# Attention in blocks of 256, 128, 128, 128, 128 and 256 tokens instead of four of 256, in a two-layer mLSTM and retention trunk

## The chip, the core and the metric

The kernel runs on one core of a Trainium2 chip. The metric is the device time of one execution in microseconds (us); the time before is the median of three runs.

## The reference, cut

Each of two layers normalises `x` (1024 tokens, width 1024), projects it with one wide matrix, runs eight heads of width 256 side by side (four mLSTM heads, four retention heads), gates and joins their outputs, and projects back onto `x`.

```python
h = rmsnorm(x, norm_g[l]) * (1.0 + scale) + shift
p = h @ w_in[l]                                   # q, k, v, gates of all heads
# mLSTM head, a step over a block of tokens j:
s   = einsum(q_j, k_j) * w_intra                  # scores inside the block, causal
num = einsum(s, v_j) + w_inter * einsum(C, q_j)   # inside the block + the state
den = sum(s) + w_inter * einsum(n, q_j)
h_j = num / maximum(abs(den), exp(-m_row))
C   = decay * C + einsum(w_end, v_j, k_j)         # the state goes to the next block
# retention head: the same with fixed decays gamma^(t-s), and no den
y   = concat(y_m, y_r) @ w_out[l]
x   = x + gate * y
```

The result does not depend on the size of the blocks. A larger block has more scores and fewer state updates.

## The kernel before

**Products.** All products are made of two halves of each operand, a high part H and a low part L. `mm3` (L133 to L136) issues three matmuls for one product: H by H (L134), L by H (L135) and H by L (L136). The halves are made by `split_to` (ScalarE writes the high part at L602; VectorE or GpSimd the low part at L603).

**Order of the work.** TensorE executes in the order of the program; the order on the other engines is made by a scheduler. The projections are cut into units of 12 matmuls with 512 columns. `run_units` issues one unit after another, and after each it gives one step (a tick) to the generators that are due, among them `attention` of the head whose projections are ready. So the attention of a head is laid between the projections of the next, a tick at a time. The projections accumulate in the PSUM pool `pp`, the attention in the pool `pa` (`ps_a()`, four tiles of 128 x 512 in f32).

**Attention of one head.** There are four blocks of CH = 256 tokens, each of two tiles of P = 128. `kT` and `qT` hold the transposed keys and queries, `kt` the key rows, `vs` the values, each as a pair of halves. For each block j:

- `scores(j)` (from L747): ten matmuls into one tile `ps`. Six make keys of the first tile by queries of both (256 columns). Four make the diagonal of the second tile (L760): one half of the keys by the two halves of the queries side by side, which gives two parts of 128 columns that are added later. VectorE multiplies both parts by the decay mask `dmat` (L762, L763), adds the two parts of the diagonal (L765), and the result is split into `sH` and `sL`. mLSTM heads make the mask from a row that is loaded (`dm_load`), cut by GpSimd and put through an exponential (`dm_make`); retention heads have a constant one, `rmask`.
- `values(j)` (L792): for each tile, the queries by the state (`cH`, `cL`, written by the update before; for j = 0 there is none), and the scores by the values. Then the normalisation of the head's output, in small VectorE, GpSimd and ScalarE steps.
- `update(j)` (L772), for j = 0, 1, 2: the new part of the state, twelve matmuls; VectorE adds it to the decayed state `cf` (L788), ScalarE and VectorE split that into `cH` and `cL`. There is one buffer of each.
- `finish(j)`: the transpose and the stores.

The order of the ticks is: loads of the masks, masks, `scores(0)`, `scores(1)`, and then for each j: `values(j)`; `update(j)`; `scores(j+2)`; `finish(j)`. A tick stands between each two. In all there are 16 heads (eight in each of two layers).

**Gates.** `gate_chain` makes, once in each layer, the columns `wi`, `we` and `dc` that weigh state and keys of the mLSTM heads, from the running maximum at the end of each block, which is loaded with one DMA into `ME` (L500) and subtracted on VectorE (L520 to L522).

Of the kernel before, what the change touches and what calls it, by code (L numbers as in the profile page):

```python
# [35 lines left out]
BIG = 1e30  # L36
GAMMA = [1.0 - 2.0 ** (-5.0 - h) for h in range(NH)]
# [32 lines left out]
def tile_hybrid_trunk(ctx, tc, x, c, positions, w_ada, b_ada, norm_g, w_in, conv_w, conv_b,  # L70
# [367 lines left out]
    def gate_chain(l, pgs, gt):  # L438
# [59 lines left out]
        ME = wt("ME", 16, 1)  # L498
        M4 = ME.rearrange("p (h j) -> p h j", h=4)
        Q.dma_start(M4, mdr[l].rearrange("h (j c) -> h j c", c=CH)[:, :, CH - 1:CH].rearrange("h j o -> o h j")  # L500
                    .to_broadcast([P, 4, 4]))
# [13 lines left out]
        wi = wd[:, 0:24].rearrange("p (h j t) -> p h j t", h=4, j=3)  # L515
        we = wd[:, 24:48].rearrange("p (h j t) -> p h j t", h=4, j=3)
        dc = wd[:, 48:56].rearrange("p (h j) -> p h j", h=4)
        for h in range(NH):
            me = M4[:, h, 0:3].unsqueeze(2).to_broadcast([P, 3, 2])
            V.tensor_tensor(wi[:, h], me, C4[:, 2:8, 2, h].rearrange("p (j t) -> p j t", t=2), ALU.subtract)  # L520
            V.tensor_tensor(we[:, h], C4[:, 0:6, 0, h].rearrange("p (j t) -> p j t", t=2), me, ALU.subtract)
        V.tensor_tensor(dc, M4[:, :, 0:2], M4[:, :, 1:3], ALU.subtract)  # L522
        A.activation(wd[:, 0:56], wd[:, 0:56], AF.Exp)
# [53 lines left out]
    def v_split(hg, gt, src, j):  # L577
        h, ml = hg % 4, hg < 4
        vH, vL = bt(F32R, 516), bt(F32R, 516)
        vH3 = vH.rearrange("p (a b) -> p a b", a=2)  # L580
        vL3 = vL.rearrange("p (a b) -> p a b", a=2)
        for tt in range(2):
            o = src[:, tt * HD:(tt + 1) * HD]
            if ml:
                s = gt["eul4"][:, h, 2 * j + tt, 0:1]
            else:
                s = kc[:, C_GS + 2 * h + tt:C_GS + 2 * h + tt + 1]
            A.activation(vH3[:, tt, 0:HD], o, AF.Copy, scale=s)
            V.scalar_tensor_tensor(vL3[:, tt, 0:HD], o, s, f(vH3[:, tt, 0:HD]), ALU.mult, ALU.subtract)
        if ml:  # L590
            for dst, src in ((vH3, gt["eH"]), (vL3, gt["eL"])):
                V.tensor_copy(dst[:, :, HD:HD + 2],
                              f(src.rearrange("p (h t o) -> p h t o", h=4, o=2)[:, h, 2 * j:2 * j + 2, :]))
        return vH3, vL3
# [41 lines left out]
    def k_rows(l, hg, j, kt, gt):  # L636
        h, ml = hg % 4, hg < 4
        half = j // 2
        a = 2 if half else 4
        kr = wt("acc", 512, 4)  # L640
        src = kdr[l][hg][half].rearrange("(b i) t -> i b t", i=32)
        for tb in range(4):
            o = tb * a * 32 + (j % 2) * 64
            Q.dma_start(kr[tb * 32:(tb + 1) * 32, :].rearrange("i (b c) -> i b c", c=64), src[:, :, o:o + 64])
        yield 2
        k3 = kr.rearrange("p (b t c) -> p t b c", t=2, c=32)
        kH, kL = bt(F32R), bt(F32R)
        kt[j] = (kH.rearrange("p (a b) -> p a b", a=2), kL.rearrange("p (a b) -> p a b", a=2))
        if ml:
            for tt in range(2):  # L650
                s = gt["we"][:, h, j, tt:tt + 1]
                dH, dL = (x[:, tt, :].rearrange("p (b c) -> p b c", c=32) for x in kt[j])
                A.activation(dH, k3[:, tt], AF.Copy, scale=s)
                V.scalar_tensor_tensor(dL, k3[:, tt], s, f(dH), ALU.mult, ALU.subtract)
        else:
            gw = float(np.float32(GAMMA[h] ** CH))
# [67 lines left out]
    def attention(l, hg, gt, qT, kT, kt, vs, gp, rot):  # L724
# [8 lines left out]
        def dm_load(j):  # L733
            if ml and j < NCH:
                dm = dms[j] = wt("dm", 512, 2)[:, 0:384]
                Q.dma_start(dm[:, 0:256], mdr[l][h:h + 1, j * CH:(j + 1) * CH].to_broadcast([P, CH]))
                Q.dma_start(dm[:, 256:384], mdr[l][h:h + 1, j * CH + P:(j + 1) * CH].to_broadcast([P, P]))

        def dm_make(j):
            if ml and j < NCH:  # L740
                dm = dms[j]
                G.affine_select(dm[:, 0:256], dm[:, 0:256], [[1, 256]], ALU.is_ge, BIG, base=0, channel_multiplier=-1)
                G.affine_select(dm[:, 256:384], dm[:, 256:384], [[1, 128]], ALU.is_ge, BIG, base=0, channel_multiplier=-1)
                for tt, sl in ((0, slice(0, 256)), (1, slice(256, 384))):
                    A.activation(dm[:, sl], dm[:, sl], AF.Exp, scale=-1.0, bias=gt["C4"][:, 2 * j + tt, 0, h:h + 1])

        def scores(j):  # L747
# [3 lines left out]
            pd = ps[:, CH:2 * CH].rearrange("p (a b) -> p a b", a=2)  # L751
            for dt in range(2):
                kk, qq = kT[dt][half], qT[dt][j]
                ks = slice(jo, jo + P)
                mm3(ps[:, 0:CH], (kk[0][:, ks], kk[1][:, ks]), (qq[:, 0:CH], qq[:, CH:2 * CH]), dt == 0, dt == 1)
            for dt in range(2):
                kk = kT[dt][half]
                qd = qT[dt][j].rearrange("p (a b) -> p a b", a=2)[:, :, P:CH]
                for i in range(2):
                    PE.matmul(pd, kk[i][:, jo + P:jo + CH], qd, start=dt == 0 and i == 0, stop=dt == 1 and i == 1)  # L760
            sd = wt("th", 512, 5)
            V.tensor_tensor(sd[:, 0:CH], ps[:, 0:CH], dmat[:, 0:CH], ALU.mult)  # L762
            V.tensor_tensor(sd[:, CH:2 * CH].rearrange("p (a b) -> p a b", a=2), pd,  # L763
                            dmat[:, CH:CH + P].unsqueeze(1).to_broadcast([P, 2, P]), ALU.mult)
            V.tensor_tensor(sd[:, CH:CH + P], sd[:, CH:CH + P], sd[:, CH + P:2 * CH], ALU.add)  # L765
            sd = sd[:, 0:CH + P]
            sH, sL = wt("sH", 384, 2, F32R), wt("sL", 384, 2, F32R)
            split_to((sH, sL), sd)
            sds[j] = (sH, sL)
            dm_load(j + 2)  # L770

        def update(j):  # L772
            if j == 0:
# [3 lines left out]
            new = (cH.rearrange("p (a b) -> p a b", a=2), cL.rearrange("p (a b) -> p a b", a=2))  # L777
            for dt in range(2):
                pu = ps_a()
                for tt in range(2):  # L780
                    kk = kt[j]
                    mm3(pu[:, 0:W], (kk[0][:, tt, dt * P:(dt + 1) * P], kk[1][:, tt, dt * P:(dt + 1) * P]),
                        (vs[j][0][:, tt, 0:W], vs[j][1][:, tt, 0:W]), tt == 0, tt == 1)
                if j == 0:
                    A.copy(cf[:, dt, 0:W], pu[:, 0:W])
                else:
                    dec = gt["dc"][:, h, j - 1:j] if ml else float(np.float32(GAMMA[h] ** CH))
# [4 lines left out]
        def values(j):  # L792
            half, jo = j // 2, (j % 2) * CH
            state = st["state"]
            sH, sL = sds[j]
            nd3 = wt("nd", 516, 1).rearrange("p (a b) -> p a b", a=2) if ml else None
            src = []
            for tt in range(2):
                pi = None
                if j > 0:  # L800
                    pi = ps_a()
                    for dt in range(2):
                        qq = qT[dt][j]
                        mm3(pi[:, 0:W], (qq[:, tt * P:(tt + 1) * P], qq[:, CH + tt * P:CH + (tt + 1) * P]), (state[0][:, dt, 0:W], state[1][:, dt, 0:W]),
                            dt == 0, ml and dt == 1)
                    if ml:
                        A.activation(nd3[:, tt, 0:W], pi[:, 0:W], AF.Copy, scale=gt["wi"][:, h, j - 1, tt:tt + 1])
                acc = not ml and j > 0
                po = pi if acc else ps_a()
                for si in range(tt + 1):  # L810
                    so = (tt * P if si == 0 else 256)
                    mm3(po[:, 0:W], (sH[:, so:so + P], sL[:, so:so + P]),
                        (vs[j][0][:, si, 0:W], vs[j][1][:, si, 0:W]), si == 0 and not acc, si == tt)
                if ml:
# [4 lines left out]
                    src.append(nd3[:, tt, 0:HD])  # L819
                else:  # L820
                    src.append(po[:, 0:HD])

            st6 = wt("st6", 12, 2)
            mv = wt("mv", 4, 2)
            mv3 = mv.rearrange("p (a b) -> p a b", a=2)
            for tt in range(2):
                V.bn_stats(st6[:, 6 * tt:6 * tt + 6], src[tt])
                V.bn_aggr(mv3[:, tt, :], st6[:, 6 * tt:6 * tt + 6])
            va = wt("va", 2, 2)
            rs = wt("rsd", 2, 2)  # L830
            if ml:
                den = nd3[:, :, HD]
# [9 lines left out]
            else:  # L842
                V.tensor_tensor(va, mv3[:, :, 1], kc[:, C_EPS + 2 * h:C_EPS + 2 * h + 2], ALU.add)
                G.tensor_tensor(rs, va, mhalf[:, 0:2], ALU.pow)
            nmu = wt("nmu", 2, 2)
            V.scalar_tensor_tensor(nmu, mv3[:, :, 0], -1.0, rs, ALU.mult, ALU.mult)
            n3 = wt("n", 512, 1).rearrange("p (a b) -> p a b", a=2)
            for tt in range(2):
                A.activation(n3[:, tt, :], src[tt], AF.Identity, scale=rs[:, tt:tt + 1], bias=nmu[:, tt:tt + 1])
            nrm[j] = n3  # L850
# [27 lines left out]
        for j in range(NCH):  # L878
            values(j)
            yield 1  # L880
            dm_make(j + 2)
            if j < NCH - 1:
                update(j)
# [3 lines left out]
            yield 1  # L887
            finish(j)
# [360 lines left out]
```

## Time and profile before

| What | Value |
|---|---|
| Time, median of three runs | 2331.36 us (2330.65 to 2338.51) |
| The profiled execution: time / span on the core | 2335.7 us / 2334.0 us |
| TensorE matmul: busy, share, instructions | 2293.4 us, 98%, 12589 |
| VectorE: busy, share, instructions | 1304.7 us, 56%, 2747 |
| ScalarE: busy, share, instructions | 889.3 us, 38%, 1736 |
| GpSimd: busy, share, instructions | 825.8 us, 35%, 801 |
| DMA | 260.50 MB, mean 112 GB/s |

In the profile PE is TensorE's matmuls, PEld its weight loads, DVE is VectorE, ACT ScalarE, POOL GpSimd and SP the engine that issues most DMAs. A row of the timeline has the start in us from the beginning of the span, the duration in us, the engine, the line of the kernel, the operation, the output and the input, the shape and the count; a square bracket holds the time that the engine stood idle before it and what ended the idle. A row of groups has the busy time in us, the mean of one instruction in ns, and behind the bar the idle time before them. A row of waits has the instruction that waited, what ended the wait, the sum in us, how often, and the longest. The span holds idle and busy time of each engine; the time of the execution is the span and a little around it.

### The profile page before, as it was taken

The page shows a single profiled execution, that of the slowest core. Times are in us where ns is not written, and L with a number is a line of the kernel's source. Part 1 is how long each engine was busy: PE and PEld are TensorE (multiplying, and loading weights), DVE is VectorE, ACT ScalarE, POOL GpSimd, SP SyncE. Part 2 cuts the span into 40 slices and gives each one's busy share as a digit, 9 for nine tenths or more (in the row PEclk, how much of TensorE's full clock was granted, in tenths as well). Part 3 has the DMA queues.
Part 4 walks back from the last instruction along what each step waited for, and adds up shares of the span by engine and source line. Part 5 has one row for each costly group of instructions (what it writes and reads, how often), then busy time and mean ns, then how long its engine had stood idle before and what let it go on. Part 6 is the DMA issues. An engine that isn't in the chain of part 4 may idle for free.

```text
span 2334.0 us, 34387 instructions
## 1 busy us (share of the span) xinstructions
PE 2293.4 (98%) x12589; PEld 1975.6 (85%) x12589; DVE 1304.7 (56%) x2747; ACT 889.3 (38%) x1736; POOL 825.8 (35%) x801
## 2 busy tenths in 40 slices
PE   6999999999999999999999999999999999999998
PEld 4888888889988888888888889888898888988886
DVE  7476687556554555574536655454553444556753
ACT  5535433433332323343434544343343322324432
POOL 1344333433333334222552434233334333341313
PEclk9999999999999999999999999999999999999999
DMA  7223332324442533385532332323223233435762
GB/s 254 76 67 95 78 84 75 97 65 116 121 115 76 149 84 96 119 261 198 179 89 61 82 77 75 84 73 76 75 71 95 73 91 86 131 90 180 263 203 81
DMA packets 326970, 260.50 MB, mean 112 GB/s; under 512 B 75892, under 2 KB 262012, under 8 KB 326800
## 3 DMA queue, kind: packets, MB, share of 16 engines
q1 hardware_dynamic: 326800, 258.30, 38.3%
q8 instruction: 99, 1.62, 0.3%
q14 instruction: 71, 0.58, 0.1%
HBM read 202.61 MB, written 55.61 MB: 111 GB/s over the span
## 4 chain that ended last, share of the span: by engine, by line
PE 87%; DVE 4%; DMA 3%; issue 2%; POOL 2%; ACT 1%; SPq 1%; POOLq 0%; ACTq 0%; DVEq 0%
PE pp L134 22%; PE pp L136 22%; PE pp L135 22%; PE pa L136 6%; PE pa L134 6%; PE pa L135 6%; PE pa L760 1%; DMA b<-in_w_ada_dram 1%; POOL wL L603 1%; DMA raw<-in_w_in_dram 1%; POOL b L603 1%; DVE acc L620 1%; DMA b<-in_x_dram 0%; POOL sL L603 0%; PE pa L304 0%
## 5 line engine op out<-in xcount | busy, mean ns | idle before, releaser
L134 PE MATMUL pp<-b,wH 128*128 128x512 f32 x1776 | 704.4, 397 | 1.8 <-ACT b L1093 1.8
L135 PE MATMUL pp<-b,wH 128*128 128x512 f32 x1776 | 701.2, 395 | 1.7 <-DVE b L1096 1.7
L136 PE MATMUL pp<-b,wL 128*128 128x512 f32 x1776 | 701.3, 395 | 0.6 <-POOL wL L603 0.6
L603 POOL TENSOR_TENSOR wL<-raw,wH 128x512 fp32r<-128x512 f32 x338 | 449.5, 1337 | 562.2 <-ACT wH L602 517.3
L136 PEld LDWEIGHTS pp<-b,wL 128*128 128x128 f32 x1776 | 334.8, 189 | 80.3 <-POOL wL L603 1.5
L135 PEld LDWEIGHTS pp<-b,wH 128*128 128x128 f32 x1776 | 334.7, 188 | 73.7 <-DVE b L1096 3.3
L134 PEld LDWEIGHTS pp<-b,wH 128*128 128x128 f32 x1776 | 334.9, 189 | 72.5 <-ACT b L1093 2.7
L602 ACT CAST wH<-raw 128x512 fp32r<-128x512 f32 x402 | 246.2, 617 | 381.5 <-PE pp L136 116.3
L134 PE MATMUL pp<-wH,b 128*128 128x256 f32 (+1 forms) x1152 | 352.7, 306 | 0.0
L136 PE MATMUL pp<-wH,b 128*128 128x256 f32 (+1 forms) x1152 | 352.3, 306 | 0.0
L135 PE MATMUL pp<-wL,b 128*128 128x256 f32 (+1 forms) x1152 | 352.3, 306 | 0.0
L603 POOL TENSOR_TENSOR b<-acc,b 128x256 fp32r<-128x256 f32 (+1 forms) x208 | 202.2, 992 | 337.0 <-ACT b L602 321.9
L136 PEld LDWEIGHTS pp<-wH,b 128*128 128x128 f32 x1152 | 216.5, 188 | 11.5
L134 PEld LDWEIGHTS pp<-wH,b 128*128 128x128 f32 x1152 | 216.9, 188 | 10.8
L135 PEld LDWEIGHTS pp<-wL,b 128*128 128x128 f32 x1152 | 216.7, 188 | 10.9
L602 ACT CAST b<-acc 128x256 fp32r<-128x256 f32 (+1 forms) x208 | 93.7, 487 | 193.6 <-DVE acc L697 138.7
L620 DVE SCALAR_TENSOR_TENSOR acc<-pp,cols,acc 128x511 f32<-128x511 f32 (+2 forms) x192 | 142.7, 743 | 44.2 <-ACT acc L615 42.0
L603 POOL TENSOR_TENSOR sL<-th,sH 128x384 fp32r<-128x384 f32 x64 | 67.8, 1059 | 249.4 <-ACT sH L602 148.9
L134 PE MATMUL pa<-wH,b 128*128 128x512 f32 x256 | 101.1, 395 | 0.0
L136 PE MATMUL pa<-wH,b 128*128 128x512 f32 x256 | 100.9, 394 | 0.0
L135 PE MATMUL pa<-wL,b 128*128 128x512 f32 x256 | 100.9, 394 | 0.0
L624 ACT ACTIVATE th<-acc 128x512 f32<-128x512 f32 x64 | 40.5, 632 | 148.6 <-DVE acc L622 76.7
(249 smaller groups left out, 3447.5 us busy)
## 6 DMA issues: line engine op xcount, KB each, us to landing
raw<-in_w_in_dram SPq DMA_DIRECT2D x274, 256.0 KB
raw<-in_w_out_dram SPq DMA_DIRECT2D x128, 256.0 KB
gdr<-g SPq DMA_DIRECT2D x64, 256.0 KB
ndr<-zt SPq DMA_DIRECT2D x128, 128.0 KB
raw<-in_w_ada_dram SPq DMA_DIRECT2D x64, 256.0 KB
g<-gdr SPq DMA_DIRECT2D x64, 256.0 KB
acc<-ndr SPq DMA_DIRECT2D x64, 256.0 KB
acc<-kdr SPq DMA_DIRECT2D x192, 64.0 KB
```

Of the source, the lines that this page charges most:

```text
L134: PE.matmul(o, lt[0], rt[0], start=start, stop=False)
L135: PE.matmul(o, lt[0], rt[1], start=False, stop=False)
L136: PE.matmul(o, lt[1], rt[0], start=False, stop=stop)
L602: A.copy(dst[0], src)
L603: eng.tensor_tensor(dst[1], src, f(dst[0]), ALU.subtract)
L620: V.scalar_tensor_tensor(acc[:, d:], pt[:, 0:HALF - d], wcol, acc[:, d:], ALU.mult, ALU.add)
L624: A.activation(th, acc, AF.Tanh, scale=0.5)
L760: PE.matmul(pd, kk[i][:, jo + P:jo + CH], qd, start=dt == 0 and i == 0, stop=dt == 1 and i == 1)
```

## The change

Blocks 0 and 3 stay whole (`WHOLE`). Blocks 1 and 2 are treated as two blocks of 128 tokens each, so that there are six blocks in a head.

- The score tile between the two halves of blocks 1 and 2 is not made; the second half takes the first from the state instead. Both halves of such a block are diagonals, of four matmuls each, into the two halves of one `ps` tile; the multiply by the mask follows each diagonal, then come two adds.
- `update` takes a tuple of tiles and is called five times in a head: for both tiles of block 0, and for each tile of blocks 1 and 2.
- `values` and the normalisation take the tiles of their block together or one by one. For blocks 1 and 2 the order of the ticks is: `values` of the first tile and its `update`; `scores(j+2)`; `values` of the second tile and its `update`; `finish(j)`. The number of ticks is the same.
- The gate columns are made for each tile of 128 instead of each block of 256 (`ME` has 32 columns instead of 16), the exponential of `wd` runs over 64 columns instead of 56, with five VectorE subtractions in place of nine. The second piece of the mask row is loaded only for whole blocks, and the mask of a split block is 128 + 128 columns instead of 256 + 128.
- The constant weights of keys, values and normalisation in the retention heads follow the shorter blocks (`place`, `span`).

```diff
+WHOLE = (0, 3)
+
+def place(t):
+    return t % 2 if t // 2 in WHOLE else 0
+
+def span(j):
+    return CH if j in WHOLE else P
...
-        ME = wt("ME", 16, 1)
+        ME = wt("ME", 32, 1)
...
-        for h in range(NH):
-            me = M4[:, h, 0:3].unsqueeze(2).to_broadcast([P, 3, 2])
-            V.tensor_tensor(wi[:, h], me, C4[:, 2:8, 2, h].rearrange("p (j t) -> p j t", t=2), ALU.subtract)
-            V.tensor_tensor(we[:, h], C4[:, 0:6, 0, h].rearrange("p (j t) -> p j t", t=2), me, ALU.subtract)
-        V.tensor_tensor(dc, M4[:, :, 0:2], M4[:, :, 1:3], ALU.subtract)
-        A.activation(wd[:, 0:56], wd[:, 0:56], AF.Exp)
+        V.tensor_tensor(wi[:, :, 0:5], M4[:, :, 1:6], peak[:, :, 2:7], ALU.subtract)
+        V.tensor_tensor(wi[:, :, 5:6], M4[:, :, 5:6], peak[:, :, 7:8], ALU.subtract)
+        V.tensor_tensor(we[:, :, 0:1], low[:, :, 0:1], M4[:, :, 1:2], ALU.subtract)
+        V.tensor_tensor(we[:, :, 1:6], low[:, :, 1:6], M4[:, :, 1:6], ALU.subtract)
+        V.tensor_tensor(dc, M4[:, :, 1:5], M4[:, :, 2:6], ALU.subtract)
+        A.activation(wd, wd, AF.Exp)
...
-                Q.dma_start(dm[:, 256:384], mdr[l][h:h + 1, j * CH + P:(j + 1) * CH].to_broadcast([P, P]))
+                if j in WHOLE:
+                    Q.dma_start(dm[:, 256:384], mdr[l][h:h + 1, j * CH + P:(j + 1) * CH].to_broadcast([P, P]))
...
+        def diagonal(pd, j, tt):
+            o = (j % 2) * CH + tt * P
+            for dt in range(2):
+                kk = kT[dt][j // 2]
+                qd = qT[dt][j].rearrange("p (a b) -> p a b", a=2)[:, :, tt * P:(tt + 1) * P]
+                for i in range(2):
+                    PE.matmul(pd, kk[i][:, o:o + P], qd, start=dt == 0 and i == 0, stop=dt == 1 and i == 1)
...
         def scores(j):
             ps = ps_a()
             sd = wt("th", 512, 5)
             if j in WHOLE:
...
+            else:
+                s4 = sd.rearrange("p (t a b) -> p t a b", t=2, a=2)
+                for tt in range(2):
+                    pd = ps[:, tt * CH:(tt + 1) * CH].rearrange("p (a b) -> p a b", a=2)
+                    diagonal(pd, j, tt)
+                    m = dmat[:, tt * P:(tt + 1) * P] if ml else dmat[:, CH:CH + P]
+                    V.tensor_tensor(s4[:, tt], pd, m.unsqueeze(1).to_broadcast([P, 2, P]), ALU.mult)
+                s3 = sd[:, 0:CH].rearrange("p (t b) -> p t b", t=2)
+                V.tensor_tensor(s3[:, 0], s4[:, 0, 0], s4[:, 0, 1], ALU.add)
+                V.tensor_tensor(s3[:, 1], s4[:, 1, 0], s4[:, 1, 1], ALU.add)
+                n = CH
...
-        def update(j):
+        def update(tiles):
...
-                for tt in range(2):
+                for t in tiles:
...
-                    dec = gt["dc"][:, h, j - 1:j] if ml else float(np.float32(GAMMA[h] ** CH))
+                    dec = gt["dc"][:, h, tiles[0] - 2:tiles[0] - 1] if ml else float(np.float32(GAMMA[h] ** P))
...
-        def values(j):
+        def values(j, tts):
...
+                sources = [(tt, tt * P)]
+                if j in WHOLE:
+                    sources = [(si, 256 if si else tt * P) for si in range(tt + 1)]
...
         for j in range(NCH):
-            values(j)
-            yield 1
+            whole = j in WHOLE
+            values(j, (0, 1) if whole else (0,))
+            if whole:
+                yield 1
             dm_make(j + 2)
             if j < NCH - 1:
-                update(j)
+                update((2 * j, 2 * j + 1) if whole else (2 * j,))
             yield 1
             if j + 2 < NCH:
                 scores(j + 2)
             yield 1
+            if not whole:
+                values(j, (1,))
+                update((2 * j + 1,))
+                yield 1
             finish(j)
             yield 1
```

More of the change, by code (lines that the diff above doesn't have):

```diff
@@ L586, in v_split @@
             else:
-                s = kc[:, C_GS + 2 * h + tt:C_GS + 2 * h + tt + 1]
+                s = kc[:, C_GS + 2 * h + place(2 * j + tt):C_GS + 2 * h + place(2 * j + tt) + 1]
             A.activation(vH3[:, tt, 0:HD], o, AF.Copy, scale=s)
@@ L655, in k_rows @@
         else:
-            gw = float(np.float32(GAMMA[h] ** CH))
+            gw = float(np.float32(GAMMA[h] ** span(j)))
             dH, dL = (x.rearrange("p (t b c) -> p t b c", t=2, c=32) for x in (kH, kL))
@@ L750, in scores @@
             ps = ps_a()
[L751 to L760, printed above, removed]
@@ L761, in scores @@
-            sd = wt("th", 512, 5)
[L762 to L768, printed above, removed]
@@ L769, in scores @@
-            sds[j] = (sH, sL)
+            sd = wt("th", 512, 5)
+            if j in WHOLE:
+                pd = ps[:, CH:2 * CH].rearrange("p (a b) -> p a b", a=2)
+                for dt in range(2):
+                    kk, qq = kT[dt][half], qT[dt][j]
+                    ks = slice(jo, jo + P)
+                    mm3(ps[:, 0:CH], (kk[0][:, ks], kk[1][:, ks]), (qq[:, 0:CH], qq[:, CH:2 * CH]), dt == 0, dt == 1)
+                diagonal(pd, j, 1)
+                V.tensor_tensor(sd[:, 0:CH], ps[:, 0:CH], dmat[:, 0:CH], ALU.mult)
+                V.tensor_tensor(sd[:, CH:2 * CH].rearrange("p (a b) -> p a b", a=2), pd,
+                                dmat[:, CH:CH + P].unsqueeze(1).to_broadcast([P, 2, P]), ALU.mult)
+                V.tensor_tensor(sd[:, CH:CH + P], sd[:, CH:CH + P], sd[:, CH + P:2 * CH], ALU.add)
+                n = CH + P
+            else:
[9 more added lines that the diff above has]
+                n = CH
@@ L770, in scores @@
+            s2 = (wt("sH", 384, 2, F32R)[:, 0:n], wt("sL", 384, 2, F32R)[:, 0:n])
+            split_to(s2, sd[:, 0:n])
+            sds[j] = s2
             dm_load(j + 2)
-        def update(j):
-            if j == 0:
+        def update(tiles):
+            j, first = tiles[0] // 2, tiles[0] == 0
+            if first:
                 st["cf"] = wt("cf", 516, 1).rearrange("p (a b) -> p a b", a=2)
@@ L790, in update @@
             st["state"] = new
-        def values(j):
-            half, jo = j // 2, (j % 2) * CH
+        def values(j, tts):
             state = st["state"]
             sH, sL = sds[j]
-            nd3 = wt("nd", 516, 1).rearrange("p (a b) -> p a b", a=2) if ml else None
-            src = []
-            for tt in range(2):
+            if tts[0] == 0:
+                st["nd"] = wt("nd", 516, 1).rearrange("p (a b) -> p a b", a=2) if ml else None
+                nrm[j] = wt("n", 512, 1).rearrange("p (a b) -> p a b", a=2)
+            nd3 = st["nd"]
+            src = {}
+            for tt in tts:
                 pi = None
@@ L803, in values @@
                         qq = qT[dt][j]
-                        mm3(pi[:, 0:W], (qq[:, tt * P:(tt + 1) * P], qq[:, CH + tt * P:CH + (tt + 1) * P]), (state[0][:, dt, 0:W], state[1][:, dt, 0:W]),
-                            dt == 0, ml and dt == 1)
+                        mm3(pi[:, 0:W], (qq[:, tt * P:(tt + 1) * P], qq[:, CH + tt * P:CH + (tt + 1) * P]),
+                            (state[0][:, dt, 0:W], state[1][:, dt, 0:W]), dt == 0, ml and dt == 1)
                     if ml:
-                        A.activation(nd3[:, tt, 0:W], pi[:, 0:W], AF.Copy, scale=gt["wi"][:, h, j - 1, tt:tt + 1])
+                        A.activation(nd3[:, tt, 0:W], pi[:, 0:W], AF.Copy,
+                                     scale=gt["wi"][:, h, 2 * j + tt - 2:2 * j + tt - 1])
                 acc = not ml and j > 0
                 po = pi if acc else ps_a()
-                for si in range(tt + 1):
-                    so = (tt * P if si == 0 else 256)
+                sources = [(tt, tt * P)]
+                if j in WHOLE:
+                    sources = [(si, 256 if si else tt * P) for si in range(tt + 1)]
+                for n, (si, so) in enumerate(sources):
                     mm3(po[:, 0:W], (sH[:, so:so + P], sL[:, so:so + P]),
-                        (vs[j][0][:, si, 0:W], vs[j][1][:, si, 0:W]), si == 0 and not acc, si == tt)
+                        (vs[j][0][:, si, 0:W], vs[j][1][:, si, 0:W]), n == 0 and not acc, n == len(sources) - 1)
                 if ml:
@@ L842, in values @@
             else:
[L843 to L850, printed above, removed]
+                e = C_EPS + 2 * h + place(2 * j + a)
+                V.tensor_tensor(va, mv3[:, a:b, 1], kc[:, e:e + n], ALU.add)
+                G.tensor_tensor(rs, va, mhalf[:, 0:n], ALU.pow)
+            nmu = wt("nmu", 2, 2)[:, 0:n]
+            V.scalar_tensor_tensor(nmu, mv3[:, a:b, 0], -1.0, rs, ALU.mult, ALU.mult)
+            for i, tt in enumerate(tts):
+                A.activation(nrm[j][:, tt, :], src[tt], AF.Identity, scale=rs[:, i:i + 1], bias=nmu[:, i:i + 1])
         def finish(j):
```

49 lines of the change are left out of this document (27 added, 22 removed).

## The prediction

> **What bounds the kernel now.** I read the page first (the busy row, the granted clock, the chain that ended last), then the groups of instructions by shape, then the waits, and last the timeline around the score products.
>
> ```profile
> span 2334.0 us, 34387 instructions
> PE 2293.4 (98%) x12589; PEld 1975.6 (85%) x12589; DVE 1304.7 (56%) x2747; ACT 889.3 (38%) x1736; POOL 825.8 (35%) x801
> ...
> PEclk9999999999999999999999999999999999999999
> ...
> PE 87%; DVE 4%; DMA 3%; issue 2%; POOL 2%; ACT 1%; SPq 1%; POOLq 0%; ACTq 0%; DVEq 0%
> ```
>
> TensorE is busy for 98% of the span at the full clock, and 87% of the chain that ended last is its own. So the time is a count of matmuls times their spacing, plus whatever makes TensorE stand still. VectorE is busy for 56%: it is not the bound, but it may be late at a given place. The change works on both sides. It removes matmuls, and it alters what TensorE waits for inside a score product.
>
> **What a matmul costs.** Starts, not durations, are counted, because the matmuls overlap. The columns are start, duration, engine, line, operation, output and input.
>
> ```profile
> 183.51 0.28 PE L134 MATMUL pa<-b,b 128*128 128x256 f32 x1
> ...
> 184.21 0.63 PE L760 MATMUL pa<-b,b 128*128 128x256 f32 x4
> 184.68 0.40 PE L134 MATMUL pp<-b,wH 128*128 128x512 f32 x1
> ...
> 200.38 0.39 PE L134 MATMUL pp<-b,wH 128*128 128x512 f32 x1
> ...
> 205.95 0.28 PE L134 MATMUL pa<-cH,b 128*128 128x258 f32 x1
> ```
>
> The ten matmuls of one `scores` take 184.68 − 183.51 = 1.17 us, so 0.117 us each; the four of the diagonal take 184.68 − 184.21 = 0.47 us. The 24 projection matmuls from 200.38 to 205.95 are two units: 5.57 us, 0.232 us each.
>
> **Matmuls removed.** Per head, `scores` had 4 × (6 + 4) = 40. Now the outer blocks keep 10 and the inner two have two diagonals of 4: 36. `values` had 9 in block 0 and 21 in each other block (12 on the state, 9 on three score tiles): 72. The inner blocks lose the off-diagonal score tile, three matmuls each: 66. `update` had three times 12; now it is 12 and four times 6: the same 36. So 148 becomes 138, and over 16 heads 160 go: 160 × 0.117 to 0.12 = **−19 us**, all of it on the engine that bounds.
>
> **A wait that is added inside scores.** This is the step that I hold to decide. In the kernel before, TensorE issues all ten matmuls, and only then does VectorE read the result (L762). In the changed kernel the inner blocks issue a diagonal, then VectorE's multiply of it, then the second diagonal, and both diagonals lie in one PSUM tile of 512 columns. In the order of the changed kernel the first matmul of the second diagonal waits for the count that this multiply raises, in all 32 inner blocks (two in each of 16 heads). TensorE works in program order, so behind that matmul stand the rest of the scores and every projection matmul; behind those stand the evacuations that VectorE and ScalarE feed on. How late VectorE is at that place can be read from the kernel before, where its lateness cost nothing:
>
> ```profile
> L762 DVE TENSOR_TENSOR th<-pa,dm x32: 409/418/430, 186.9 to 1724.6; 128x256 f32<-128x256 f32 x32
> L762 DVE TENSOR_TENSOR th<-pa,rmask x32: 411/420/426, 661.7 to 2155.9; 128x256 f32<-128x256 f32 x32
> ...
>   PE pa L760: 28.2, 11
> ```
>
> Of 64 such multiplies 11 waited for TensorE. The other 53 found the ten matmuls long done: VectorE came later. The first and the last inner block, and one where VectorE did stand waiting:
>
> ```profile
> 189.21 0.16 DVE L592 CAST b<-eL 128x4 fp32r<-128x4 f32 x1
> ...
> 189.48 0.41 DVE L762 TENSOR_TENSOR th<-pa,dm 128x256 f32<-128x256 f32 x1
> ```
> ```profile
> 2138.71 0.75 DVE L912 SCALAR_TENSOR_TENSOR b<-g,cols,b 128x512 fp32r<-128x512 f32 x1
> 2139.37 0.42 DVE L762 TENSOR_TENSOR th<-pa,rmask 128x256 f32<-128x256 f32 x1
> ```
> ```profile
> 2037.49 0.43 DVE L762 TENSOR_TENSOR th<-pa,rmask 128x256 f32<-128x256 f32 x1 [2.21 <-PE pa L760]
> ```
> ```profile
> 2036.12 0.28 PE L134 MATMUL pa<-b,b 128*128 128x256 f32 x1
> ...
> 2036.82 0.64 PE L760 MATMUL pa<-b,b 128*128 128x256 f32 x4
> 2037.29 0.39 PE L134 MATMUL pp<-b,wH 128*128 128x512 f32 x1
> ...
> 2136.64 0.28 PE L134 MATMUL pa<-b,b 128*128 128x256 f32 x1
> ```
>
> The scores of the first inner block begin at 183.51 and the multiply at 189.48, 5.97 us later, with VectorE at work on the gate and key rows until then. In the last they begin at 2136.64, the multiply at 2139.37, 2.73 us later. Now TensorE would issue four matmuls (0.47 us) and stand until the multiply ends (0.42 us after its start). The stall is lateness + 0.42 − 0.47: 5.92 us in the first, 2.68 us in the last. Where VectorE already waits, the multiply starts 2037.49 − 2037.29 = 0.20 us after the fourth matmul's slot ends, so the floor is 0.20 + 0.43 = 0.63 us. By this rule, row by row, the 32 give 89 us: mLSTM blocks 1 and 2 20.5 and 29.5 us, retention 20.4 and 18.3 us. Five lie at the floor, ten are over 3.4 us. What VectorE executes ahead of the multiply is nearly the same in both orders, which is why I carry its lateness over. The bounds are 32 × 0.63 = 20 us (VectorE is there each time) and, with as much again as a few instructions put in front of it, 95 us. I take **+85 us**, near the rows: after one stall VectorE and TensorE are level, so the head's second one begins with a little less backlog.
>
> The Trainium skill ("PSUM — Partial Sum Buffer", the rule on bank collisions) asks for PSUM to be guarded by bank and not by address, since a TensorE write and a VectorE read in one bank are an error. It speaks against this change: by its table of terms the tile is one bank, so the wait is needed though the two halves do not overlap; no run here shows such a collision.
>
> **The clock after a stall.** TensorE's clock falls after idle time:
>
> ```profile
> 983.80 0.39 PE L136 MATMUL pp<-b,wL 128*128 128x512 f32 x1
> 985.12 0.39 PE L134 MATMUL pa<-b,sH 128*128 128x256 f32 x1 [0.94 <-ACT sH L602]
> ...
> 986.32 0.39 PE L136 MATMUL pa<-b,sL 128*128 128x256 f32 x1 [0.69 <-POOL sL L603]
> ...
> 987.96 0.63 PE L136 MATMUL pp<-b,wL 128*128 128x512 f32 x1
> 988.39 0.63 PE L134 MATMUL pp<-b,wH 128*128 128x512 f32 x1
> ```
> ```profile
> 987.40:990.80 3.40, 3.40 (x10) 2.64 (x9) 1.41 (x6) 1.02 (x2) 1.35 (x2) 0.51 0.24 88
> 2127.50:2130.90 3.40, 3.40 (x13) 2.92 (x12) 1.40 (x6) 0.56 (x2) 1.71 (x2) 0.50 0.40 147
> ```
>
> From 983.80 to 986.32 three matmuls are issued, which takes 0.58 us unhindered (0.23, 0.23 and 0.12); the other 1.94 us TensorE stands. In the second fence, windows of the trace, the granted clock stands behind the busy times of the five engines: it is 0.51 for 3.4 us afterwards, and the 512-column spacing is 0.43 instead of 0.232 us. One drop costs half of 3.4, 1.7 us. Twenty of the 32 stalls are over 1.94 us. A drop begins on a grid of 3.4 us (the two here are 1140.1 us, 334 such steps, apart), so a stall that straddles a step is split; weighted by length I expect 17 drops. The two shown go (next part), so 15 more: **+25 us**, bounds 8 to 20 in all: +10 to +31.
>
> The Trainium skill ("TensorE: Matmul & The Clock Gate", Part 1) puts the half rate after at least one idle window of some 3.4 us; the row above shows less than that to suffice, and here the measurement decides. By the page the sum would be 11 us less.
>
> **Waits that go.** `values(0)` follows `scores(1)` and today waits for block 0's split scores:
>
> ```profile
> PE pa L136 <- POOL sL L603: 3.0, 5, 0.7
> ...
> PE pa L134 <- ACT sH L602: 1.9, 2, 0.9
> PE pa L134 <- ACT cH L602: 1.0, 1, 1.0
> ...
> PE pa L135 <- DVE cL L603: 0.3, 1, 0.3
> ```
>
> While TensorE stands in `scores(1)`, ScalarE and GpSimd finish those: 3.0 + 1.9 = **−5 us**. They come back if the stall goes.
>
> **Five state updates.** Each adds two state adds and a split:
>
> ```profile
> L788 DVE SCALAR_TENSOR_TENSOR cf<-cf,wd,pa 128x258 f32<-128x258 f32 x32 | 13.9, 471 | 0.0
> L602 ACT CAST cH<-cf 128x516 fp32r<-128x516 f32 x24 | 14.9, 622 | 16.1 <-DVE cf L788 15.9
> L603 DVE TENSOR_TENSOR cL<-cf,cH 128x516 fp32r<-128x516 f32 x24 | 17.6, 731 | 11.6 <-ACT cH L602 11.6
> L765 DVE TENSOR_TENSOR th<-th 128x128 f32<-128x128 f32 x64 | 26.3, 411 | 1.3
> ```
>
> VectorE gains 2 × (2 × 0.47 + 0.73) = 3.3 us a head, 53 us in all, and 32 more adds of 0.41 us, 13 us: 1305 + 66 is 59% of the span, beside TensorE's work. On the path is only the chain: last update matmul, state add, cH, cL, next `values` on the state, 2 × 0.47 + 0.62 + 0.73 = 2.3 us bare. Today three ticks cover it and it costs 1.0 + 0.3 us once (the cH and cL rows). At two places a head only two units now cover it, 5.57 us. If VectorE stayed as late as in its worst places, some 20 us would appear; but after a stall its backlog is gone. Bounds 0 to 15; I take **+2 us**, nearest to the rows of today.
>
> **At nothing.** The gate columns: one DMA of twice the columns, and five subtractions for nine.
>
> ```profile
>   DVE wd L522: 4.5, 2
> ```
> ```profile
> 148.83 0.15 DVE L521 TENSOR_TENSOR wd<-COL,ME 128x6 f32<-128x6 f32 x1
> ...
> 185.50 0.87 DVE L654 SCALAR_TENSOR_TENSOR b<-acc,wd,b 128x256 fp32r<-128x256 f32 x2
> ```
>
> VectorE's wait on that DMA is 4.5 us over the two layers, and the last subtraction stands 36 us ahead of the first reader, the key rows at 185.50, with projections between; without that cover it would cost the 4.5 us. Sixteen decay-row DMAs leave SP's queue, and GpSimd's mask selects and split scores shrink (256 instead of 384 columns): less on queues that hold nobody up here, except through sL, counted above. Retention's normalisation per tile adds small VectorE and GpSimd steps behind `values`; the VectorE ones come behind the state split in the order.
>
> **Sum.** −19 + 85 + 25 − 5 + 2 = +88 us. The profiled execution took 2335.7 us (span 2334.0 and 1.7 around it), 4.3 over the median of the runs. 2335.7 + 88 = 2423.7 profiled, **2419 us** as a median. Ends: −19 + 54 (half of what lies above the floor) + 10 − 5 + 0 = +40, 2371; −19 + 95 + 31 − 5 + 15 = +117, 2449.
>
> **Rivals.** *VectorE is there at once:* the scheduler puts the first multiply ahead of the backlog, and each stall is at the floor. −19 + 20 − 5 + 2 = −2: 2329 us, no change. For it: 11 of 64 multiplies waited today. Against: the rest did not, by up to 6 us.
>
> *Faster:* the wait costs nothing, because the matmuls before it are still running when the multiply ends, and the saving is left: −19 + 2 = −17, 2314 us. It decides when the stalls sum below 5 us, 0.17 us each. Against: the multiply alone lasts 0.42.
>
> *The clock falls only after a whole idle window of 3.4 us:* then the ten stalls over that give 10 × 1.7 = 17, less 3.4 for the two that go: 14 instead of 25, 2408 us. Against: the drops at 987.4 and 2127.5. This is the rule of the Trainium skill's clock gate page named above.
>
> *Longer:* every stall drops the clock (32 × 1.7 = 54, less 3 for the two there are) and the state chain is late where it was late before (+20): −19 + 89 + 51 − 5 + 20 = +136, 2467 us.
>
> **How the numbers follow.** Forecast 0.74, VectorE at once 0.08, faster 0.05, clock after a whole window 0.06, longer 0.07. The range 2371 to 2449 holds the forecast and the clock rival, 0.80. What a measurement of this kernel tells from no change is 0.5%, 11.7 us: faster below 2319.7, slower above 2343. So slower is 0.74 + 0.06 + 0.07 = 0.87, the same 0.08, faster 0.05.
>
> **What the profile of the changed kernel would show.** Idle of TensorE before the second diagonal, ended by VectorE's th multiply, 32 times and 70 to 95 us; granted clock at half in some 17 stretches of 3.4 us inside the attention; 160 fewer matmuls; waits for cH and cL of a few us; waits for sH and sL nearly gone. I am wrong if that idle sums below 40 us, if the clock does not fall, or if cH and cL hold TensorE for over 15 us.

## The result, and the profile after

| | before | changed |
|---|---|---|
| median | 2332.8 us (4 runs, 2330.7 to 2338.5) | 2401.6 us (4 runs, 2400.0 to 2404.7) |
| ratio | 1 | 1.0291, 95% interval 1.0278 to 1.0304 |
| span of the profiled execution | 2334.0 us | 2400.0 us |

The change makes the kernel slower by 69 us; the forecast was 88 us, from 2331 to 2419.

The head of the page of the changed kernel:

```profile
span 2400.0 us, 34320 instructions
PE 2295.8 (96%) x12429; PEld 1970.7 (82%) x12429; DVE 1366.4 (57%) x2899; ACT 908.5 (38%) x1768; POOL 823.1 (34%) x817
```

160 matmuls are gone (12429 for 12589), and the span is still 66 us longer. The waits of TensorE in the changed kernel (what waited, what ended it, sum in us, times, longest), those above 1 us:

```profile
PE pa L765 <- DVE th L790: 68.6, 32, 5.8
PE pa L251 <- DVE b L246: 9.9, 2, 9.2
PE pa L315 <- ACT b L308: 6.1, 3, 5.6
PE pa L220 <- DMA rows<-in_c_dram: 2.7, 1, 2.7
PE pp L145 <- ACT b L1137: 1.8, 2, 1.1
PE pp L146 <- DVE b L1140: 1.7, 3, 0.9
PE pa L146 <- DVE cL L615: 1.5, 4, 0.5
PE pa L765 <- ACT n L888: 1.3, 1, 1.3
```

The first row is new: the diagonal matmuls (L765) wait for the mask multiply (L790) 32 times. Rows two to six belong to the first 72 us and stand in the kernel before as well. The rows for sH and sL of the kernel before are gone. The first inner block on TensorE and on VectorE:

```profile
183.54 0.63 PE L765 MATMUL pa<-b,b 128*128 128x256 f32 x4
189.95 1.22 PE L765 MATMUL pa<-b,b 128*128 128x256 f32 x4 [5.78 <-DVE th L790]
190.97 0.63 PE L145 MATMUL pp<-b,wH 128*128 128x512 f32 x1
191.39 0.63 PE L146 MATMUL pp<-b,wH 128*128 128x512 f32 x1
```
```profile
189.49 0.41 DVE L790 TENSOR_TENSOR th<-pa,dm 128x256 f32<-128x256 f32 x1
```

Four matmuls, then nothing for 5.8 us, until VectorE reaches the multiply at 189.49. In the kernel before it reached it at 189.48. So VectorE came no earlier for the wait. After the wait the matmuls of 512 columns are 0.42 us apart, and the windows show why (length, busy times of the five engines with TensorE's and its weight loads first, then the granted clock):

```profile
184.00:189.90 5.90, 0.17 (x2) 0.00 (x0) 5.68 (x14) 3.35 (x9) 1.03 (x1) 0.95 0.59 179
191.00:194.40 3.40, 3.40 (x10) 2.63 (x10) 0.72 (x2) 0.40 (x1) 1.40 (x4) 0.50 0.31 65
455.00:461.80 6.80, 4.02 (x22) 3.27 (x21) 3.86 (x9) 3.42 (x8) 1.27 (x1) 1.00 0.14 39
```

VectorE is busy for 5.68 of the 5.90 us in which TensorE stands. Then the granted clock is 0.50. The third row holds a stall of 2.94 us (another inner block) after which the clock stayed at 1.00.

To account for the 66 us between the two profiled spans (the medians differ by 69) I took the time from each matmul's start to the next and subtracted the undisturbed spacing of its width (0.2325 us for 512 columns, 0.118 for 256, 0.1215 for 258). What is left is sorted by what ended the wait, or by the half clock:

| Term | before | changed | difference | predicted |
|---|---|---|---|---|
| undisturbed spacing of all matmuls after 72 us | 2236.9 | 2217.9 | −19.0 | −19 |
| waits for the multiply inside scores | 0 | 73.7 | +73.7 | +85 |
| half clock | 3.3 | 15.4 | +12.1 | +25 |
| waits for sH and sL | 6.0 | 0 | −6.0 | −5 |
| waits for cH and cL | 1.8 | 2.1 | +0.4 | +2 |
| all else (small lengthenings, other waits, startup) | | | +5 | 0 |
| sum | | | +66 | +88 |

### The profile page after: what moved, and what is told of

The parts are those of the page before. It is cut to its first block, busy times and chain, and to the rows that moved or that the text cites. A ratio compares the mean times of both kernels' runs of the same rounds, so it can differ in the third digit from the quotient of the medians.

```text
span 2400.0 us, 34320 instructions
## 1 busy us (share of the span) xinstructions
PE 2295.8 (96%) x12429; PEld 1970.7 (82%) x12429; DVE 1366.4 (57%) x2899; ACT 908.5 (38%) x1768; POOL 823.1 (34%) x817
## 5 line engine op out<-in xcount | busy, mean ns | idle before, releaser
L615 POOL TENSOR_TENSOR sL<-th,sH 128x384 fp32r<-128x384 f32 (+1 forms) x64 | 57.8, 904 | 228.9 <-ACT sH L614 173.5
L765 PE MATMUL pa<-b,b 128*128 128x256 f32 x384 | 68.8, 304 | 69.9 <-DVE th L790 68.6
L765 PEld LDWEIGHTS pa<-b,b 128*128 128x128 f32 x384 | 57.4, 201 | 79.4 <-DVE th L790 75.1
```

Of the source, the lines that this page charges most:

```text
L615: eng.tensor_tensor(dst[1], src, f(dst[0]), ALU.subtract)
L765: PE.matmul(pd, kk[i][:, o:o + P], qd, start=dt == 0 and i == 0, stop=dt == 1 and i == 1)
```

## The experiments

The theory: TensorE stands inside the split scores, because the second diagonal shares a PSUM tile with the first, which VectorE is still to multiply. Its main rival: five state updates and more VectorE work cost the time, and the wait in the middle only shows it.

**Both diagonals first, then both multiplies.**

```diff
-for tt in range(2):
-    pd = ps[:, tt * CH:(tt + 1) * CH]...
-    diagonal(pd, j, tt)
-    m = ...
-    V.tensor_tensor(s4[:, tt], pd, m..., ALU.mult)
+for tt in range(2):
+    diagonal(pds[tt], j, tt)
+for tt in range(2):
+    m = ...
+    V.tensor_tensor(s4[:, tt], pds[tt], m..., ALU.mult)
```

> The changed kernel, but in the two split blocks both diagonals are issued first and the two mask multiplies after them; everything else of the change stays. Theory (TensorE stands inside the split scores for the first multiply): the 32 idles ended by the th multiply go to zero, with them the 73.7 us that they lengthen the changed kernel and most of its 15 us at half clock; some 6 us of waits for sH and sL come back. The median falls from 2402 to 2310 to 2325 us, under the kernel before (2333) by up to the 19 us of the removed matmuls. Rival (the five state updates and the added VectorE work cost the time): the order of two multiplies changes little, 2380 us or more.

Measured: 2322.1 us, 0.9949 of the kernel before (0.9937 to 0.9962), 80 us under the changed kernel. The groups of this kernel, diagonal matmuls and their idle time:

```profile
L765 PE MATMUL pa<-b,b 128*128 128x256 f32 x384 | 55.9, 281 | 2.0 <-ACT n L889 2.0
```

The same row of the changed kernel:

```profile
L765 PE MATMUL pa<-b,b 128*128 128x256 f32 x384 | 68.8, 304 | 69.9 <-DVE th L790 68.6 <-ACT n L888 1.3
```

The waits for the multiply are gone, the mean of one matmul falls from 304 to 281 ns, and half clock costs 2 us by the same account. Everything else of the change, the five updates too, is still in it. The rival falls.

**The same order, but two PSUM tiles.**

```diff
-pd = ps[:, tt * CH:(tt + 1) * CH].rearrange(...)
+pd = (ps if tt == 0 else ps_a())[:, 0:CH].rearrange(...)
```

> The changed kernel with its order of instructions kept (diagonal, multiply, diagonal, multiply), but the second diagonal goes into a PSUM tile of its own. Theory (the wait comes from the shared PSUM tile): the 32 idles go although the order stays, 2310 to 2335 us; the extra tile in a pool of four may bring a new wait for a free tile, up to 15 us, which would show as idle of TensorE ended by VectorE or ScalarE on pa. Rival (the order of the multiply is what holds TensorE, whatever the tile): the idles stay near 70 us and the time near 2400 us.

Measured: 2321.9 us, 0.9946 (0.9931 to 0.9961). No diagonal waits for the multiply; the largest sum of waits of TensorE after the startup is this one:

```profile
PE pa L147 <- POOL sL L615: 3.6, 4, 1.1
```

So neither the order nor the number of tiles matters by itself: the wait needs both, a multiply issued between two matmul groups, and one tile under both. The extra tile brought no wait of its own: the one wait of a diagonal for ScalarE's n (1.7 us by the account) stands in the changed and in the reordered kernel too, with 1.4 and 2.1 us, and the one wait for the multiply of a whole block (th L780, 2.3 us), which the changed kernel does not have, stands in the reordered kernel too, with 2.2 us. The Trainium skill ("PSUM — Partial Sum Buffer", the rule on bank collisions) asks for a guard by bank, not by address. This run agrees as far as it goes: with a tile for each half there is no such wait. Whether the wait hangs on the tile or on the bank under it, no run here tells.

**The wait alone, in the kernel before.** In blocks 1 and 2 the multiply of the first 256 columns is moved ahead of the diagonal.

```diff
+sd = wt("th", 512, 5)
+if j in (1, 2):
+    V.tensor_tensor(sd[:, 0:CH], ps[:, 0:CH], dmat[:, 0:CH], ALU.mult)
 for dt in range(2):        # the four diagonal matmuls
     ...
-sd = wt("th", 512, 5)
-V.tensor_tensor(sd[:, 0:CH], ps[:, 0:CH], dmat[:, 0:CH], ALU.mult)
+if j in (0, 3):
+    V.tensor_tensor(sd[:, 0:CH], ps[:, 0:CH], dmat[:, 0:CH], ALU.mult)
```

> The kernel before, with one line moved: in blocks 1 and 2 the mask multiply of the first 256 columns is issued ahead of the diagonal, which lies in the same PSUM tile; nothing else of the change. Theory: this alone brings 32 idles of TensorE ahead of the diagonal, each shorter by the two further matmuls that stand ahead of it (0.24 us) where VectorE is late: 60 to 75 us, with 8 to 20 us at half clock, less 6 us of waits that go: 2385 to 2425 us. Rival (the wait costs little by itself, and the time comes from the six blocks): 2333 to 2350 us.

Measured: 2432.6 us, 1.0423 (1.0409 to 1.0438). One moved line costs 98 us, more than the whole change and 8 us over the expected range.

```profile
PE pa L763 <- DVE th L758: 76.1, 32, 5.9
```

By the account the 32 waits lengthen it by 81.3 us and half clock by 26 instead of 3 us. This is the closest test of the prediction's rule for a stall (lateness of VectorE in the kernel before, plus the multiply, less the matmuls that stand ahead): six matmuls ahead instead of four take 0.235 us from each of the 27 places above the floor, so the rule gives 83 us for this kernel, and 81 were measured. Single places miss by more, in both directions: one of 4.5 us by the rule measured 2.7, another of 5.0 measured 6.1. The order of VectorE's instructions is not quite the same in this kernel either. I had expected 60 to 75 because I scaled the rule down by what the changed kernel showed. That was wrong: the changed kernel's smaller sum is, for the most part, a matter of its own order on VectorE (below).

**The wait in block 2 only.** The reordered kernel, with the changed kernel's order kept for block 2.

```diff
 diagonal(pds[0], j, 0)
+if j == 2:
+    masked(0)
 diagonal(pds[1], j, 1)
+if j == 1:
+    masked(0)
 masked(1)
```

> The changed kernel, with the reordered multiplies in block 1 and the changed kernel's own order in block 2. Theory: 16 idles are left. In the changed kernel the 16 of block 2 sum to 41 us and those of block 1 to 32 us, so the time lies above that of the fully reordered kernel by 41 us and some 6 us of half clock, somewhat more if the stall in block 1 had let VectorE catch up: 2350 to 2380 us. Rival (the idles only show time that would be lost anyway): within 15 us of the fully reordered kernel or of the changed one.

Measured: 2369.6 us, 1.0153 (1.0140 to 1.0167), 47.5 us above the reordered kernel.

```profile
PE pa L765 <- DVE th L790: 35.5, 16, 5.4
```

By the account 38 us of waits and 13 instead of 2 us of half clock: 49 us. In the changed kernel the 16 places of block 2 held 41 of the 74 us. Kept alone they bring back 47.5 of the 79.5 us between the reordered and the changed kernel, so the loss is a sum over places, as the prediction priced it.

**The clock by itself.** A kernel that leaves out the whole computation: bursts of 40 to 52 matmuls with chains of VectorE instructions of twelve lengths between them.

```diff
+for g in range(96):
+    for i in range(40 + (7 * g) % 13):
+        PE.matmul(ps, first if i == 0 else w, m, ...)
+    V.tensor_tensor(t, ps, one, ALU.mult)
+    k, small = divmod(g % 12, 2)
+    ...   # k more of 512 columns, and one of 128 where small is 1
+    V.tensor_copy(first, t[:, 0:P])
```

> A kernel that leaves out the whole computation: 96 bursts of 40 to 52 matmuls of 512 columns, and after each a chain of VectorE instructions that TensorE waits for, of twelve lengths in turn, estimated from the rows of this kernel at 0.95 to 4.3 us. It measures by itself what the prediction priced at 25 us and the changed kernel paid some 12 us for: which idle drops the granted clock. Theory A (the share of idle within one window of 3.4 us on a fixed grid decides, at about 1.9 us): no drop after idles under 1.8 us, a drop after some of those of 2 to 3.6 us depending on where the grid cuts them, after all of those over 3.8 us. Theory B (a whole window of 3.4 us must be idle): no drop under 3.4 us and after at most a quarter of those of 3.4 to 4.3 us.

Measured in one execution, from the starts of its matmuls (idle: from the end of the last matmul's slot to the next start); the idles came out at 1.2 to 5.2 us:

| idle, us | 1.20 | 1.52 | 1.92 | 2.25 | 2.65 | 2.98 | 3.38 | 3.71 | 4.10 and more |
|---|---|---|---|---|---|---|---|---|---|
| clock fell, of 8 each | 0 | 0 | 1 | 4 | 4 | 5 | 7 | 7 | 31 of 31 |

Two idles of the same length, with opposite ends (windows: each idle, and the 3.1 us behind it):

```profile
50.10:52.20 2.10, 0.08 (x1) 0.00 (x0) 1.88 (x4) 0.00 (x0) 1.00 0.00 0
52.30:55.40 3.10, 3.10 (x7) 2.48 (x8) 0.00 (x0) 0.00 (x0) 0.50 0.00 0
590.60:592.70 2.10, 0.08 (x1) 0.00 (x0) 1.88 (x4) 0.00 (x0) 1.00 0.00 0
592.80:595.90 3.10, 3.10 (x14) 2.56 (x15) 0.00 (x0) 0.00 (x0) 1.00 0.00 0
```

After the same 2.25 us, seven matmuls fit into 3.1 us in one case and 14 in the other (ScalarE has no column here, so the clock stands behind GpSimd's). A grid of 3.414 us with one phase for the whole run, both fitted to this trace, separates all 95 idles: where the idle inside one window of it was 1.93 us or more the clock fell, where it was 1.87 us or less it did not. Theory A holds. Theory B, the whole idle window of the Trainium skill's page on the clock gate ("TensorE: Matmul & The Clock Gate", Part 1), does not agree with this trace: 2.25 us sufficed four times.

**Where the rest of the 19 us stays.** The reordered kernel is 12.7 us under the kernel before, not 19. Its own waits of TensorE:

```profile
PE pa L147 <- POOL sL L615: 3.6, 4, 1.1
...
PE pa L146 <- DVE cL L615: 2.8, 7, 0.7
PE pa L145 <- DVE th L780: 2.0, 1, 2.0
PE pa L765 <- ACT n L889: 2.0, 1, 2.0
PE pa L145 <- ACT sH L614: 1.9, 2, 0.9
```

By the account cH and cL cost 2.2 us more than in the kernel before, the multiply of a whole block (th L780) 2.2 us more and n 1.5 us more; sL costs 0.5 us more and sH the same. Two edits on it. First, in split blocks the update's matmuls and state add go ahead of the values; only the split into cH and cL stays behind them (the code is condensed):

```diff
-    values(j, (0,)); dm_make(j + 2); update((2 * j,))
+    update((2 * j,)); values(j, (0,)); new_state(); dm_make(j + 2)
```

> The reordered kernel (both diagonals, then the multiplies), and in the split blocks the update's matmuls and its state add stand ahead of the values instead of behind them; only the split of the state follows the values. It asks where some 6 of the 19 us of removed matmuls stay in the reordered kernel. Theory (the state chain of five updates is covered by only two units): the idles ended by cL, 4.0 us in seven places there, go below 1.5 us, and the time falls by 2 to 5 us to 2317 to 2320. Rival (VectorE is simply late there, and the order of the matmuls does not matter): the same idles, within 2 us of 2322.

Measured: 2316.5 us, 0.9927 (0.9913 to 0.9941). TensorE has no wait for cL any more, and the median is 5.5 us under that of the reordered kernel. The runs of the two overlap (2314.7 to 2323.5 us here, 2319.2 to 2324.1 there), and the profiled execution is the slowest of its four, 2323.5 us, with 6 us at half clock: the trace shows that the wait is gone, the gain stands on the medians alone. Second, two ticks instead of one between the scores of block 1 and the values of block 0:

```diff
-        yield 2 if hg == 0 else 1
+        yield 2
```

> The reordered kernel, with two ticks instead of one between the scores of block 1 and the values of block 0 in all heads but the first, which has them already. Theory (TensorE waits at the values of block 0 for the split scores sH and sL, 6.5 us in six places there, and one clock drop of 1.7 us): these go, and the time falls by 4 to 8 us to 2314 to 2318. Rival (every later step comes a tick later, and the heads collide elsewhere): no gain or a loss.

Measured: 2316.5 us, 0.9925 (0.9910 to 0.9940).

```profile
PE pa L765 <- ACT n L889: 3.0, 1, 3.0
...
PE pa L147 <- POOL sL L615: 1.7, 2, 1.1
...
PE pa L145 <- ACT nd L840: 1.6, 1, 1.6
PE pa L146 <- DVE cL L615: 1.1, 3, 0.5
```

The waits for sL halve and those for sH go, as does most of the wait for th L780. A part comes back as waits of `pa` tiles for ScalarE (n 3.0 us instead of 2.0, nd new). Both together:

> The reordered kernel with both edits, the update ahead of the values in split blocks and two ticks ahead of the values of block 0. If both gains are independent they add: 6 to 12 us under the reordered kernel, 2310 to 2316 us. If they compete for the same time of VectorE, no more than the larger of the two.

Measured: 2322.1 us, 0.9944 (0.9932 to 0.9957): no better than without either. Its waits show new ones for n:

```profile
PE pa L145 <- ACT n L892: 4.1, 2, 2.1
```

The waits for cL and sL are smaller than in the reordered kernel. This does not account for the whole difference of 5.5 us to each edit alone; since single runs of one kernel lie up to 9 us apart (2314.7 to 2323.5 for the first edit), what remains is left open. Each single edit gives a version that beats both kernels, by 18 us the one before and by 85 us the changed one.

## Why the prediction was right, point by point

**Matmuls removed** was exact: 160 fewer and −19.0 us of undisturbed spacing. It is also the whole of what the change can gain; the reordered kernel keeps 12.7 us of it, and 18 us with either of the two later edits.

**The wait inside scores** was right in place, count and mechanism: 32 waits, at the second diagonal, ended by the multiply. Its size was 73.7 us instead of 85. Row by row, the mLSTM heads agree (blocks 1 and 2: 19.8 and 28.2 us, 20.5 and 29.5 forecast); the retention heads do not (12.6 and 13.2 us, 20.4 and 18.3 forecast). The step that failed there is "what VectorE executes ahead of the multiply is nearly the same in both orders". In the last layer's first retention head, block 1, before and after:

```profile
1811.70 0.69 DVE L531 SCALAR_TENSOR_TENSOR g<-th,pp 128x512 f32<-128x512 f32 x1 [2.49 <-ACT th L529]
1812.31 0.42 DVE L762 TENSOR_TENSOR th<-pa,rmask 128x256 f32<-128x256 f32 x1
```
```profile
1867.38 0.42 DVE L790 TENSOR_TENSOR th<-pa,rmask 128x256 f32<-128x256 f32 x1 [1.13 <-PE pa L765]
1868.75 0.69 DVE L543 SCALAR_TENSOR_TENSOR g<-th,pp 128x512 f32<-128x512 f32 x1 [0.94 <-ACT th L541]
```

Before, the multiply stood behind a gate instruction that waited 2.49 us for ScalarE. After, the scheduler put it in front of that, so VectorE was there at once and the stall fell to the floor of 0.68 us (0.63 forecast, without some 0.05 us of restart). Six retention places, forecast at 1.6 to 2.7 us each, fell to the floor like this; in all six VectorE now waits for TensorE ahead of the multiply, 0.60 to 1.13 us. They make up 9.9 of the 15 us by which the rows (89 us) missed. The rival "VectorE is there at once" was thus true for some places: 12 of the 32 lie at the floor, where five were forecast. In the kernel before with the wait alone added, the place shown keeps its stall (2.42 us, 2.36 by the rule).

**The clock after a stall** was right in kind and too large, 12.1 us for 25. There were nine drops, not 17, so the step that failed is the count. Their mean price, 15.4 / 9 = 1.7 us, is the forecast one, but by luck: it is a mean of two kinds. Six lasted one step of 3.4 us and cost 1.5 to 1.6 us each. The other three lasted 6.8, 6.8 and 10.2 us and cost 2.7 to 2.9 us each (with the shorter matmuls counted too, which the table's row leaves out). The second step of a long drop, and the 3.3 us behind a short one (windows as above):

```profile
192.80:196.10 3.30, 3.30 (x10) 2.52 (x9) 0.00 (x0) 0.00 (x0) 1.29 (x4) 0.50 0.49 93
588.80:592.10 3.30, 3.30 (x16) 2.69 (x15) 1.89 (x2) 0.62 (x1) 1.61 (x2) 1.00 0.22 79
```

In the first case the half clock began at 189.35 us, 0.60 us before the stall ended; in the second at 585.29, 0.21 us before. In these nine a further step at half clock followed where the stall ran 0.60 us or more into a step, and none where it ran 0.40 us or less into it. So the prediction's price for a drop is that of a short one.

For the count: only 13 stalls were over 1.94 us instead of 20, since the stalls were smaller; and of those the four between 2.4 and 3.2 us were all cut by the grid into parts of 1.77 to 1.95 us, near or below the limit that the clock kernel puts between 1.87 and 1.93 us. In the clock kernel nine of 16 idles of 2.65 and 2.98 us made it fall, so here the phase was kind. The rival with the whole idle window was priced at 14 us net, nearer to the 12 measured, and by the lengths of its stalls the changed kernel cannot tell the two rules apart: its nine drops follow the nine stalls of 3.6 us and more. But one of them, at 813.99 us, began behind a window with 2.1 us of idle only, in the kernel with the wait in block 2 only stalls of 2.4 and 3.0 us dropped the clock, and the clock kernel excludes that rival.

**Waits that go** held: 6.0 for 5 us, and as the text said they come back without the stall, with 4.3 us for sL and 2.2 us for sH in the reordered kernel and in the one with two tiles. **Five state updates** came out small, 0.4 for 2 us. The cover that the text gave for it, a backlog gone after a stall, is not shown: without the stalls the waits for cL are 4.0 us in the reordered kernel, but 2.2 us in the one with two tiles, against 2.1 us in the changed kernel.

**All else** was taken as nothing and is 5 us, mostly small lengthenings of under 0.25 us each (6.7 for 1.5 us). The starts in the trace name two kinds: 24 times a diagonal matmul right behind a stall takes 0.22 instead of 0.118 us to the next start, 2.5 us in all, and 24 matmuls of 256 columns inside the half-clock stretches make another 2.3 us.

**Two small slips** of the prediction change nothing: the upper end, 2331.4 + 117, is 2448 and not 2449, and the first reader of the gate columns behind the exponential is ScalarE's L653 at 184.0 us, 1.5 us ahead of the row shown.

## What to carry to other kernels

An instruction of another engine that reads a PSUM tile between two matmul groups into the same tile makes an in-order TensorE wait for that engine's backlog (here VectorE's, 0.7 to 5.9 us at 32 places); issue both groups first or give the second a tile of its own. The lateness of a consumer that costs nothing today, the time from a producer's end to the start of its reader, can be read from the profile, and it prices the wait if the producer is ever made to depend on it: 81 us measured for 83 with the wait alone, but 74 for 89 where the change let the scheduler put the multiply ahead of older work. Compare the gain of a count (19 us for 160 matmuls) with the number of new waits times that lateness before cutting a block.

## What the runs showed of the hardware

In the clock kernel TensorE's granted clock fell to half when the idle within one window of a fixed grid of 3.414 us (fitted) was 1.93 us or more, and did not at 1.87 us or less; a stall of 2.25 us fell on either side, four times each, by where the grid cut it. All 31 idles of 4.1 us and more dropped it. The half clock lasted one step of 3.4 us, and two where the idle ran on into the first: in the clock kernel 39 drops with up to 0.57 us of idle in that step lasted one, 20 with 0.61 us or more two. In the changed kernel a drop of one step cost TensorE 1.5 to 1.6 us and a longer one 2.7 to 2.9 us, on top of the stall.
